# Layer 0's first gate and second scale vectors on TensorE, both first feed-forward chunks from x, and a GLA vector in the stage before

## The chip, the cores and the metric

One core of a Trainium2 chip runs the whole program. The engines are TensorE (PE, matrix products), VectorE (DVE), ScalarE (ACT), GpSimd (POOL) and SyncE (SP, whose queue issues the loads of weights). The metric is the device time of one execution in microseconds; lower is better. Products write to eight banks of PSUM, everything else lies in SBUF.

## The reference, cut to what matters

The model is a trunk of four residual layers for one sequence of 256 tokens of width 1024. Layers 0 and 3 mix tokens by sliding-window attention (16 query heads, 4 key heads), layer 1 by gated linear attention (GLA), layer 2 by forgetting attention. Each mixer is followed by a SwiGLU feed forward of width 2816. A vector `c` gives, per layer, six vectors of 1024: shift, scale and gate of the mixer, and shift, scale and gate of the feed forward.

```python
c_act = jax.nn.silu(c)
for i in range(DEPTH):
    mod = c_act @ ada_w[i] + ada_b[i]
    sh1, sc1, g1, sh2, sc2, g2 = jnp.split(mod, 6, axis=-1)
    h = modulate(rmsnorm(x, norm_gain[i, 0]), sh1, sc1)
    y = mixer(h)
    x = x + g1[:, None, :] * y
    h = modulate(rmsnorm(x, norm_gain[i, 1]), sh2, sc2)
    x = x + g2[:, None, :] * swiglu(h, ffn_w_gu[i], ffn_w_down[i])
return rmsnorm(x, final_norm)
```

`modulate(h, shift, scale)` is `h * (1 + scale) + shift`. All arrays are float32. In GLA each head's output of 256 columns is normalised by its own mean square before it is multiplied by a gate.

## The kernel before

**Layout.** `x` lies in SBUF with the features on partitions: eight tiles of 128 features by 256 tokens. A weight matrix comes in chunks of up to 1 MB, one DMA each, into one of five `raw` buffers. A chunk is then split into a high part `wh` (a cast on ACT, L194) and a low part `wl` (the rest, on DVE, L196), each in two pieces. The activations are split the same way (`hh`, `hl`), and a product is three matmuls, high x high, high x low and low x high (`mm3`, L277 to L279).

**The stream.** `Stream` holds one list of all chunks in the order in which they are loaded, the chunks of the `ada` matrices among them. It works through them in pieces. At every step of a product (`tick`) it does as many pieces as are due, so that the weights of the two chunks ahead (`LOOK`) are ready in time; an `ada` chunk that stands between weight chunks is worked off in its turn. A `raw` buffer is free for the next load when its last piece is done. A second generator (`bg`) feeds the steps of attention or GLA in between the same way. The order on each engine is that in which the code issues, as the framework's scheduler arranges it.

**The `ada` vectors.** A chunk gives two columns of `mod`, 256 of a vector's 1024 values. In general DVE does it: two dot products of 128x1024 with the spread-out `cact` (L213). For layer 0's first two vectors (shift and scale of the mixer) the matrix lies the other way round and PE does it in `ada_rows`: `product` multiplies with `ccol`, a column of `c` padded to 32, in eight matmuls of 128x32 by 256 columns (L228), ACT copies the resulting row (L229), and `turn` makes two columns of it with two matmuls (L233) to which DVE adds the bias (L235).

**Where the vectors stand in the stream.** `ORDER0` gives layer 0's order: h and s are shift and scale of the mixer, g its gate, H, S shift and scale of the feed forward, w a weight chunk. In the later layers `MIX_ADA` names the vectors that are loaded within the mixer, here number 4 (scale of the feed forward), and `DOWN_ADA` those that are loaded in the down projection before, number 2 (the mixer's gate); the rest goes into the gate-and-up chunks before.

**The output projection.** `out_proj` runs over two halves of the heads, in each over eight tiles of features. A tile takes a bank `mm` (three of them), twelve matmuls, and `add_x` on DVE (L514), which frees the bank.

**The feed forward's start.** The norm of `x` is not known until all of `x` is. `x_done` therefore forms, tile by tile, `uh` and `ul` = x times the norm's weights, and `first_chunk` multiplies the first chunk by these 256 columns and two of the shift; meanwhile the mean squares are summed (L326, L339), the reciprocal root is spread over partitions (L349), and `h_tiles` makes `hh` and `hl`. The result is scaled afterwards (L491). The second chunk comes from `hh` and `hl` (`proj_feat`).

**GLA.** `finish` squares a head's output on ACT into the two halves of `sq`, POOL adds the two halves (L1006), and PE sums over partitions (L1014).

## Time and profile before

| | |
|---|---|
| median of 3 runs | 1251.55 us (1249.82 to 1258.61) |
| profiled execution | 1254.5 us |
| its span, first to last instruction | 1252.7 us |
| mean granted TensorE clock | 0.987 |
| DMA | 298.51 MB, mean 238 GB/s |
| costliest DVE group, L196 `wl` | 448.4 us, 408 instructions |
| L213, the dot products of the `ada` vectors | 224.2 us, 176 instructions |

The profile gives busy time per engine, and for each idle stretch of an engine the instruction of another engine that ended it. A matmul's row in the timeline shows its length from start to end; since they overlap, the spacing of their starts tells what one costs in a row of them. `x4` at a row's end counts instructions that follow each other; a float32 matmul stands as two instructions. The windows view lists for each stretch the busy time of PE, PEld (weight loads), DVE, ACT and POOL, then the granted clock, the share of DMA time and GB/s.

### The profile page before, as it was taken

To read this page: it belongs to the slowest core of one execution; us is meant where nothing else is said; L and a number is where in the kernel's file an instruction comes from. 1 tells how busy PE (TensorE), PEld (TensorE's weight loads), DVE (VectorE), ACT (ScalarE), POOL (GpSimd) and SP (SyncE) were. 2 spreads that over 40 slices of the span, in tenths; PEclk is the share of its full clock that TensorE was granted. 3 is DMA by queue.
4 is the path that set the end of the run, shared out by engine and by line. 5 is a ranking of instruction groups with operands and counts; after the bars stand their busy time and mean duration, and the time that the engine had idled before them with its cause. 6 is when DMAs were issued, how large, how long until landed. Compare 5 with 4: busy or idle time off the path is not lost.

```text
span 1252.7 us, 19770 instructions
## 1 busy us (share of the span) xinstructions
PE 1207.5 (96%) x7444; PEld 1051.5 (84%) x7444; DVE 1001.1 (80%) x1828; ACT 697.8 (56%) x1293; POOL 133.9 (11%) x177
## 2 busy tenths in 40 slices
PE   6997899999998999999999999999999999999997
PEld 4875788888888998888889999888889979888886
DVE  3798998879779989888878668988787998666553
ACT  4474654444576666444457877645444677544442
POOL 0020110001115321000021101100011021000011
PEclk8998899999999999999999999999999999999999
DMA  9855789977744436998875543799788444656440
GB/s 355 330 196 206 269 295 347 344 269 261 267 175 162 165 137 233 355 331 292 272 270 200 202 173 132 278 351 343 266 279 280 166 153 169 225 212 214 161 163 34
DMA packets 45105, 298.51 MB, mean 238 GB/s; under 512 B 5217, under 2 KB 5377, under 8 KB 14802
## 3 DMA queue, kind: packets, MB, share of 16 engines
q1 hardware_dynamic: 44210, 295.56, 65.3%
q8 instruction: 58, 0.95, 0.3%
q10 hardware_dynamic: 432, 1.18, 0.3%
q0 software_dynamic: 368, 0.53, 0.1%
q14 instruction: 37, 0.30, 0.1%
HBM read 296.16 MB, written 1.05 MB: 237 GB/s over the span
## 4 chain that ended last, share of the span: by engine, by line
PE 85%; DVE 8%; ACT 3%; issue 2%; POOL 1%; DMA 1%; SPq 0%; DVEq 0%; ACTq 0%; POOLq 0%
PE mm L1160 13%; PE mm L277 12%; PE mm L278 12%; PE mm L279 11%; PE s L277 7%; PE s L278 7%; PE s L279 7%; PE mm L1162 7%; PE s L576 2%; DVE wl L196 2%; PE o L606 2%; DVE raw L213 2%; PE t L1131 1%; ACT wh L194 1%; PE t L617 1%
## 5 line engine op out<-in xcount | busy, mean ns | idle before, releaser
L196 DVE TENSOR_TENSOR wl<-raw,wh 128x1024 fp32r<-128x1024 f32 (+2 forms) x408 | 448.4, 1132 | 87.3 <-ACT wh L194 86.2
L194 ACT CAST wh<-raw 128x1024 fp32r<-128x1024 f32 (+2 forms) x408 | 375.9, 964 | 231.7 <-issue 105.1
L1160 PE MATMUL mm<-a,wh 128*128 128x512 f32 x704 | 247.8, 396 | 0.0
L213 DVE CUSTOM_DVE_ANT_0 raw<-raw,cact,const 128x1024 f32<-128x1024 f32 x176 | 224.2, 1292 | 16.7 <-DMA raw<-in_ada 16.5
L277 PE MATMUL mm<-wh,hh 128*128 128x512 f32 (+1 forms) x560 | 198.9, 355 | 2.2 <-ACT wh L194 1.8
L1162 PE MATMUL mm<-a,wl 128*128 128x256 f32 x704 | 198.0, 281 | 0.0
L278 PE MATMUL mm<-wl,hh 128*128 128x512 f32 (+1 forms) x560 | 194.9, 348 | 0.7 <-DVE wl L196 0.7
L279 PE MATMUL mm<-wh,hl 128*128 128x512 f32 (+1 forms) x560 | 194.6, 348 | 0.0
L1160 PEld LDWEIGHTS mm<-a,wh 128*128 128x128 f32 x704 | 132.2, 188 | 30.1
L277 PE MATMUL s<-wh,hh 128*128 128x512 f32 (+2 forms) x384 | 145.1, 379 | 2.9 <-ACT hh L454 2.9
L278 PE MATMUL s<-wl,hh 128*128 128x512 f32 (+2 forms) x384 | 143.2, 374 | 0.0
L279 PE MATMUL s<-wh,hl 128*128 128x512 f32 (+2 forms) x384 | 141.9, 373 | 0.0
L433 POOL TENSOR_TENSOR sq<-sq,sq 128x256 f32<-128x256 f32 x48 | 52.3, 1090 | 761.3 <-ACT sq L422 724.7
L1162 PEld LDWEIGHTS mm<-a,wl 128*128 128x128 f32 x704 | 133.0, 189 | 0.2
L277 PEld LDWEIGHTS mm<-wh,hh 128*128 128x128 f32 x560 | 107.1, 191 | 18.9 <-issue 3.0
L279 PEld LDWEIGHTS mm<-wh,hl 128*128 128x128 f32 x560 | 107.2, 191 | 13.9 <-issue 0.8
L278 PEld LDWEIGHTS mm<-wl,hh 128*128 128x128 f32 x560 | 107.2, 191 | 13.1 <-DVE wl L196 1.0
L514 DVE SCALAR_TENSOR_TENSOR x<-mm,mod,x 128x256 f32<-128x256 f32 x128 | 61.5, 481 | 42.9 <-PE mm L1162 35.2
L277 PEld LDWEIGHTS s<-wh,hh 128*128 128x128 f32 x384 | 72.3, 188 | 15.5 <-ACT hh L454 3.4
L277 PE MATMUL mm<-oh,wh 128*128 128x256 f32 x256 | 74.5, 296 | 9.3 <-DVE x L514 9.3
L279 PEld LDWEIGHTS s<-wh,hl 128*128 128x128 f32 x384 | 71.8, 188 | 13.1
L278 PEld LDWEIGHTS s<-wl,hh 128*128 128x128 f32 x384 | 72.3, 188 | 11.7
(220 smaller groups left out, 2005.7 us busy)
## 6 DMA issues: line engine op xcount, KB each, us to landing
raw<-in_ada SPq DMA_DIRECT2D x96, 1024.0 KB, 6.6
raw<-in_gu SPq DMA_DIRECT2D x88, 1024.0 KB, 6.1
raw<-in_down SPq DMA_DIRECT2D x64, 704.0 KB, 5.2
raw<-in_swa_in SPq DMA_DIRECT2D x12, 1024.0 KB, 6.6
raw<-in_gla_in SPq DMA_DIRECT2D x11, 1024.0 KB, 5.2
raw<-in_fox_in SPq DMA_DIRECT2D x11, 1024.0 KB, 4.9
raw<-in_swa_o SPq DMA_DIRECT2D x8, 1024.0 KB, 4.9
raw<-in_gla_o SPq DMA_DIRECT2D x4, 1024.0 KB, 4.9
```

Of the source, the lines that this page charges most:

```text
L194: nc.scalar.copy(wh[:, sl], raw[:, sl])
L196: eng.tensor_tensor(out=wl[:, sl], in0=raw[:, sl], in1=wh[:, sl].bitcast(F32), op=ALU.subtract)
L213: nc.vector.tensor_tensor_reduce(out=w, in0=w, in1=self.cact, scale=1.0, scalar=b, op0=ALU.mult, op1=ALU.add, accum_out=col)
L277: nc.tensor.matmul(out, ah, bh, start=first, stop=False)
L278: nc.tensor.matmul(out, ah, bl, start=False, stop=False)
L279: nc.tensor.matmul(out, al, bh, start=False, stop=last)
L433: (eng or nc.gpsimd).tensor_tensor(out=q, in0=self.acc, in1=q, op=ALU.add)
L514: self.nc.vector.scalar_tensor_tensor(out=self.x[:, m], in0=ps, scalar=gate[:, m:m + 1], in1=self.x[:, m], op0=ALU.mult, op1=ALU.add)
L576: nc.tensor.matmul(sc[:, so:s1], q[:, so:so + P], k[:, :k1], start=True, stop=True)
L606: nc.tensor.matmul(o[rows, b * P:S], vs[e][b], pt[:, e, :S] if b == 0 else pt[:, e, S:], start=b == 0, stop=b == 1)
L1160: nc.tensor.matmul(o, wh[:, k], a[:, kk].rearrange("p e n -> p (e n)"), start=kk == 0, stop=False)
L1162: nc.tensor.matmul(o[:, S:], wl[:, k], a[:, kk, 0], start=False, stop=kk == FT - 1)
```

## The change

It has four parts. `ROWS` extends `ada_rows` to layer 0's vectors 2 and 4 (first gate, second scale): their matrices are laid out like those of 0 and 1, and their chunks go through PE, in the mixer and the output projection, in a bank `mm` instead of `t`; `product` and `turn` are two pieces of the stream. `MIX_ADA` and `DOWN_ADA` become lists by layer: layer 1's vector 4 moves from GLA into layer 0's down projection, so SP issues its four loads there. `first_two` replaces `first_chunk` and `proj_feat` at the start of the feed forwards: both first chunks are multiplied by `uh` and `ul`, the mean squares are summed at the third step of the first chunk instead of the second, and the second half of `h_tiles` comes in the second chunk. In GLA POOL's sum goes, and PE adds both halves of the squares in one accumulation. The two attention masks become one table of four blocks in place of six, and a small tile shares the buffers of another; that makes room.

```diff
-MIX_ADA = (4,)
+MIX_ADA = ((), (), (4,), (4,))
-DOWN_ADA = (2,)
+DOWN_ADA = ((), (2, 4), (2,), (2,))
+ROWS = (0, 1, 2, 4)
...
-        if layer == 0 and nt < 2 * KT:
-            return self.ada_rows(mod[:, nt:nt + 2], bias[:, nt:nt + 2], raw)
+        if layer == 0 and nt // KT in ROWS:
+            return self.ada_rows(mod[:, nt:nt + 2], bias[:, nt:nt + 2], raw, nt < 2 * KT)
...
-        ps = self.ps("t")
-        row = self.t(self.small, [P, S], "fc", bufs=2)
+        ps = row = None
 
         def product():
+            nonlocal ps, row
+            ps = self.ps("t" if early else "mm")
+            row = self.t(self.small, [P, S], "fc", bufs=2)
...
-        return [product, lambda: self.turns.append(turn)]
+        return [product, (lambda: self.turns.append(turn)) if early else turn]
...
+    def first_two(self, names, use):
+        nc = self.nc
+        uh, ul = self.u
+        rbs = self.t(self.small, [P, S], "rbs", bufs=1)
+        for c, name in enumerate(names):
+            wh, wl = (x.rearrange("p (k n) -> p k n", k=KT) for x in self.st.get(name))
+            outs = [self.ps(("mm", "s")[c]) for _ in range(2)]
+            self.start_chunk(KT)
+            for k in range(KT):
+                for m in range(2):
+                    sl = slice(m * P, (m + 1) * P)
+                    self.mm3(outs[m][:, :S + 2], wh[:, k, sl], wl[:, k, sl], uh[:, k], ul[:, k],
+                             k == 0, k == KT - 1)
+                if c == 0 and k == 2:
+                    self.stat_start(self.acc)
+                    self.stat_end()
+                    nc.scalar.copy(rbs, self.spread(self.y))
+                    hh, hl = self.h_alloc()
+                    self.h_tiles(range(KT // 2), rbs, self.A, self.sh, hh, hl)
+                if c == 1 and k == 0:
+                    self.h_tiles(range(KT // 2, KT), rbs, self.A, self.sh, hh, hl)
+                self.tick()
+            vals = []
+            for m in range(2):
+                v = self.t(self.small, [P, S], "fc", bufs=2)
+                nc.vector.tensor_tensor(out=v, in0=outs[m][:, :S], in1=rbs, op=ALU.mult)
+                col = self.t(self.small, [P, 1], "fcol", bufs=4)
+                nc.vector.tensor_copy(col, outs[m][:, S:S + 1])
+                vals.append((v, col))
+            use(c, *vals)
+        return hh, hl
...
-            nc.gpsimd.tensor_tensor(out=sq[:, 0], in0=sq[:, 0], in1=sq[:, 1], op=ALU.add)
...
-                nc.tensor.matmul(st[:, b_:b_ + 1], sq[:, 0, b_ * P:(b_ + 1) * P],
-                                 self.c("ones")[:, 1:2], start=True, stop=True)
+                for hf in range(2):
+                    nc.tensor.matmul(st[:, b_:b_ + 1], sq[:, hf, b_ * P:(b_ + 1) * P],
+                                     self.c("ones")[:, 1:2], start=hf == 0, stop=hf == 1)
```

The next rows are DVE's order in layer 0's output projection, first half, before the change. `x_70` is x, `mod_5_74` layer 0's vectors; `L213` comes in pairs, the dot product and the read of its sum.

```order
L514 SCALAR_TENSOR_TENSOR x_70<-mm_1259,mod_5_74,x_70 128x256
L213 ISA raw_1023,mod_5_74<-raw_1023,cact_73,const_71 128x1024
L213 ISA mod_5_74 128x1
L213 ISA raw_1178,mod_5_74<-raw_1178,cact_73,const_71 128x1024
L213 ISA mod_5_74 128x1
L213 ISA raw_1178,mod_5_74<-raw_1178,cact_73,const_71 128x1024
L213 ISA mod_5_74 128x1
L514 SCALAR_TENSOR_TENSOR x_70<-mm_1278,mod_5_74,x_70 128x256
```

The same place after the change, where L214 is the dot product, L551 is `add_x`, L548 the low part of the heads' output and L238 the sum of a turned row.

```order
L238 TENSOR_TENSOR mod_5_74<-mm_1269,const_71 128x2
L551 SCALAR_TENSOR_TENSOR x_70<-mm_1290,mod_5_74,x_70 128x256
L214 ISA raw_1306,mod_5_74<-raw_1306,cact_73,const_71 128x1024
L214 ISA mod_5_74 128x1
L551 SCALAR_TENSOR_TENSOR x_70<-mm_1309,mod_5_74,x_70 128x256
L548 TENSOR_TENSOR ol_113<-o_1282,oh_112 128x256
L214 ISA raw_1306,mod_5_74<-raw_1306,cact_73,const_71 128x1024
L214 ISA mod_5_74 128x1
L551 SCALAR_TENSOR_TENSOR x_70<-mm_1331,mod_5_74,x_70 128x256
```

Between two `add_x` stands one dot product where three stood.

On PE at that place, before the change, there are the products of a tile and the transposes of attention (L617).

```order
L277 MATMUL mm_1259<-oh_112,wh_1017 128x256
L278 MATMUL mm_1259<-ol_113,wh_1017 128x256
L617 MATMUL t_1193<-const_71,pr_1135 128x128
L279 MATMUL mm_1259<-oh_112,wl_1018 128x256
L277 MATMUL mm_1259<-oh_112,wh_1017 128x256
```

After the change PE has there the product of a row (L231) and, behind five matmuls of the next tile, its turn (L236), which reads the copy `fc` that ACT makes in between.

```order
L282 MATMUL mm_1360<-oh_112,wl_1078 128x256
L231 MATMUL mm_1378<-raw_1238,ccol_97 32x256 x8
L280 MATMUL mm_1395<-oh_112,wh_1077 128x256
L281 MATMUL mm_1395<-ol_113,wh_1077 128x256
L282 MATMUL mm_1395<-oh_112,wl_1078 128x256
L280 MATMUL mm_1395<-oh_112,wh_1077 128x256
L281 MATMUL mm_1395<-ol_113,wh_1077 128x256
L236 MATMUL mm_1378<-const_71,fc_1379 128x1 x2
L282 MATMUL mm_1395<-oh_112,wl_1078 128x256
```

So a row stands between two tiles, and each row has its own place of the three banks `mm` from the product until the sum on DVE.

In layer 0's down projection DVE had this order before the change; `mod_6_75` are layer 1's vectors, 128x704 are the two pieces of a weight chunk.

```order
L196 TENSOR_TENSOR wl_2676<-raw_2540,wh_2675 128x704 x2
L514 SCALAR_TENSOR_TENSOR x_70<-mm_2628,mod_5_74,x_70 128x256 x2
L196 TENSOR_TENSOR wl_2713<-raw_2581,wh_2712 128x704 x2
L436 SCALAR_TENSOR_TENSOR ul_2590<-x_70,A_2587,uh_2589 128x256
L196 TENSOR_TENSOR wl_2751<-raw_2643,wh_2750 128x704 x2
L213 ISA raw_2726,mod_6_75<-raw_2726,cact_73,const_71 128x1024
L213 ISA mod_6_75 128x1
L213 ISA raw_2726,mod_6_75<-raw_2726,cact_73,const_71 128x1024
L213 ISA mod_6_75 128x1
```

After the change it is this (L197 is `wl`, L439 `ul`).

```order
L214 ISA raw_2822,mod_6_75<-raw_2822,cact_73,const_71 128x1024
L214 ISA mod_6_75 128x1
L439 SCALAR_TENSOR_TENSOR ul_2694<-x_70,A_2691,uh_2693 128x256
L197 TENSOR_TENSOR wl_2935<-raw_2838,wh_2934 128x704 x2
L214 ISA raw_2856,mod_6_75<-raw_2856,cact_73,const_71 128x1024
L214 ISA mod_6_75 128x1
L214 ISA raw_2856,mod_6_75<-raw_2856,cact_73,const_71 128x1024
L214 ISA mod_6_75 128x1
L551 SCALAR_TENSOR_TENSOR x_70<-mm_2883,mod_5_74,x_70 128x256
```

The dot products stand twice as close among the pieces of the weights.

More of the change, by code (lines that the diff above doesn't have):

```diff
@@ L38 @@
 CONST2_COLS = [
-    ("cos", NB * HD), ("sin", NB * HD), ("swamask", 3 * P), ("foxmask", 3 * P), ("scan", S),
+    ("cos", NB * HD), ("sin", NB * HD), ("masks", 4 * P), ("scan", S),
 ]
@@ L589, in attn_heads @@
                         nc.vector.tensor_tensor_reduce(
-                            out=sm[:, po:p1], in0=sc[:, so:s1], in1=mask[:, so:s1], scale=1.0,
+                            out=sm[:, po:p1], in0=sc[:, so:s1], in1=mask[:, 2 * P - (s1 - so):], scale=1.0,
                             scalar=BIG if ns is None else ns, op0=ALU.add, op1=ALU.min,
@@ L709, in head @@
             }
-        return self.attn_heads(pool, [head(h) for h in range(16)], self.c("swamask"), oh, ol)
+        return self.attn_heads(pool, [head(h) for h in range(16)], self.c("masks")[:, :2 * P], oh, ol)
     def pinned(self, start):
@@ L818, in few_cols @@
         nc = self.nc
-        t = self.t(self.small, [P, NB, 16], "few", bufs=1)
+        t = self.t(self.small, [P, S], "tk", bufs=3)[:, :NB * 16].rearrange("p (b n) -> p b n", b=NB)
         for b, ap in enumerate(parts):
@@ L838, in head @@
             }
-        gen = self.attn_heads(pool, [head(h) for h in range(16)], self.c("foxmask"), oh, ol)
+        gen = self.attn_heads(pool, [head(h) for h in range(16)], self.c("masks")[:, 2 * P:], oh, ol)
         for g in range(4):
@@ L1086, in gla, with gate_up_feat, use @@
         self.bg_rate = GLA_RATE[1]
-    def gate_up_feat(self, layer, j, pool, a):
+    def gate_up_feat(self, layer, pool, a):
         nc = self.nc
-        s = self.t(pool, [P, S], "st", bufs=2)
-        if j == 0:
-            self.hs, ((gv, gc), (uv, uc)) = self.first_chunk(f"g{layer}_0")
+        def use(j, gate, up):
+            (gv, gc), (uv, uc) = gate, up
+            s = self.t(pool, [P, S], "st", bufs=2)
             nc.scalar.activation(s, gv, AF.Silu, bias=gc)
             nc.vector.scalar_tensor_tensor(out=s, in0=uv, scalar=uc, in1=s, op0=ALU.add, op1=ALU.mult)
-        else:
-            g, u = self.proj_feat(self.st.get(f"g{layer}_{j}"), self.hs, "s")
-            nc.scalar.activation(s, g, AF.Silu)
-            nc.vector.tensor_tensor(out=s, in0=s, in1=u, op=ALU.mult)
-        self.split_hl(s, a[:, j, 0], a[:, j, 1], nc.gpsimd)
+            self.split_hl(s, a[:, j, 0], a[:, j, 1], nc.gpsimd)
+        self.hs = self.first_two([f"g{layer}_0", f"g{layer}_1"], use)
     def gate_up_tok(self, layer, g, pool, a, before):
@@ L1141, in ffn @@
             a = self.t(pool, [P, FT, 2, S], "a", F32R)
-            for j in range(2):
-                self.gate_up_feat(layer, j, pool, a)
+            self.gate_up_feat(layer, pool, a)
             turn = None
@@ L1232, in items @@
                 items += mix[:MIX_SPAN[0]]
-                d = sum((ada(l, v) for v in MIX_ADA), [])
+                d = sum((ada(l, v) for v in MIX_ADA[l]), [])
                 if l + 1 < DEPTH:
@@ L1239, in items @@
             if l + 1 < DEPTH:
-                done = MIX_ADA + (MIX_NEXT if l else ())
-                d1 += sum((ada(l + 1, v) for v in (1, 0, 2, 3, 4) if v not in done + DOWN_ADA), [])
-                d2 = sum((ada(l + 1, v) for v in DOWN_ADA), [])
+                done = MIX_ADA[l + 1] + DOWN_ADA[l + 1] + (MIX_NEXT if l else ())
+                d1 += sum((ada(l + 1, v) for v in (1, 0, 2, 3, 4) if v not in done), [])
+                d2 = sum((ada(l + 1, v) for v in DOWN_ADA[l + 1]), [])
             items += ff[:3]
@@ L1348, in _layout @@
     a["ada"] = ada.reshape(DEPTH * 6, 4, 2, P, D).transpose(0, 1, 3, 2, 4).reshape(DEPTH * 6, 4, P, 2 * D)
-    for v in range(2):
+    for v in ROWS:
         a["ada"][v] = _chunks(i["ada_w"][0, :, v * D:(v + 1) * D], 256)
@@ L1401, in _layout @@
     caus, full = off(kj <= qi), np.zeros((P, P), f)
-    put("swamask", np.concatenate([caus, off(kj > qi), caus], 1))
-    put("foxmask", np.concatenate([caus, full, caus], 1))
+    put("masks", np.concatenate([off(kj > qi), caus, full, caus], 1))
     put("scan", np.tile((np.arange(S) % 64 != 0).astype(f)[None], (P, 1)))
```

2 lines of the change are left out of this document (1 added, 1 removed).

## The prediction

> **What bounds the kernel now.** I read the page first, then windows of 10 us over the whole span, then the list of waits in the stretches where TensorE (PE) is not full, then the timeline there.
>
> ```profile
> span 1252.7 us, 19770 instructions
> PE 1207.5 (96%) x7444; PEld 1051.5 (84%) x7444; DVE 1001.1 (80%) x1828; ACT 697.8 (56%) x1293; POOL 133.9 (11%) x177
> PE   6997899999998999999999999999999999999997
> PEclk8998899999999999999999999999999999999999
> ```
>
> PE is the bound: it is idle for 1252.7 - 1207.5 = 45.2 us in all. So an edit can gain only where PE waits or its granted clock is down, and PE work that is added costs its full time wherever PE is full. Of the stretches that the change touches, the windows give this (columns: length, busy time of PE, PEld, DVE, ACT, POOL, granted clock, DMA share, GB/s):
>
> ```profile
> 60.10:144.20 84.10, 70.62 (x499) 57.63 (x497) 75.96 (x199) 50.78 (x138) 14.41 (x33) 0.92 0.62 226
> 984.50:1052.70 68.20, 66.87 (x532) 57.20 (x531) 61.81 (x178) 51.68 (x140) 13.77 (x33) 1.00 0.48 171
> 282.50:341.00 58.50, 57.77 (x353) 51.49 (x351) 49.52 (x74) 29.87 (x48) 7.17 (x8) 1.00 0.79 281
> 340.00:480.00 140.00, 130.58 (x1038) 125.11 (x1037) 122.44 (x289) 97.11 (x180) 36.43 (x38) 1.00 0.43 150
> ```
>
> The first is layer 0's attention and output projection, from the first transposes of the keys to the first product of its feed forward. The second is the same stretch of layer 3, which runs the same code. The third is layer 0's down projection with GLA's first chunk, the fourth GLA. In layer 0 PE is idle for 13.5 us and its clock is down for part of the rest:
>
> ```profile
> PE mm L277 <- DVE x L514: 9.4, 5, 2.6
> PE t L679 <- ACT wh L194: 3.2, 1, 3.2
> 98.00:100.00 2.00, 2.00 (x7) 1.02 (x7) 2.00 (x7) 0.69 (x2) 0.00 (x0) 0.50 0.93 393
> 134.00:136.00 2.00, 2.00 (x11) 2.00 (x11) 1.61 (x3) 1.29 (x4) 0.24 (x1) 0.50 0.98 356
> ```
>
> The large wait is for `add_x` (L514), which frees the `mm` bank that PE wants; behind it and behind the wait of 3.2 us the clock is at half. What holds VectorE (DVE) up is the dot product of the scale vectors, L213. This is its busy time in layer 3's and in layer 0's stretch (half of the instructions are the read of the accumulator):
>
> ```profile
> 984.50:1052.70 68.20, 8.99 (x14) 1.00 0.48 171
> 60.10:144.20 84.10, 27.57 (x44) 0.92 0.62 226
> ```
>
> **Layer 0's gate and second scale on PE.** Sixteen of layer 0's 24 pieces of L213 leave DVE, and eight remain, about what layer 3 has (7 in its stretch). So layer 3 shows what the stretch costs with that much DVE work. By the order of the program it has 36 more products in it (chunks that layer 0 does earlier), at the spacing of the rows below, 0.12 us: 4.3 us. Layer 0 at layer 3's pace takes 68.2 - 4.3 = 63.9 us, against 84.1: an excess of 20.2 us, which is waits, half clock and the disorder behind both. Against it stands what PE gets: eight products of 8 matmuls and eight turns of 2, which the kernel already does for the first two vectors (the first two rows are of the chain of waits, the others of the timeline; the last two are `add_x` and a piece of L213):
>
> ```profile
> 40.05 1.00 PE t L228 x16
> 41.05 0.54 PE t L233 x4
> 39.65 0.28 PE L278 MATMUL mm<-wl,hh 128*128 128x256 f32 x1
> 39.77 0.28 PE L279 MATMUL mm<-wh,hl 128*128 128x256 f32 x1
> 39.98 1.07 PE L228 MATMUL t<-raw,ccol 128*32 128x256 f32 x16
> 40.22 0.36 ACT L229 COPY fc<-t 128x256 f32<-128x256 f32 x1
> 40.98 1.14 PEld L233 LDWEIGHTS t<-const,fc 128*128 128x128 f32 x8 [0.41 <-ACT fc L229]
> 279.79 0.48 DVE L514 SCALAR_TENSOR_TENSOR x<-mm,mod,x 128x256 f32<-128x256 f32 x1 [1.43 <-PE mm L1162]
> 337.78 1.28 DVE L213 CUSTOM_DVE_ANT_0 raw<-raw,cact,const 128x1024 f32<-128x1024 f32 x1 [0.76 <-DMA raw<-in_ada]
> ```
>
> A product takes 1.00 and a turn 0.54 us. The first matmul of the product starts 0.21 us after the one ahead of it where 0.12 is usual, so entering costs 0.1 and I take as much for leaving: 1.74 us a row, 13.9 for eight. [...]
>
> That leaves 20.2 - 13.9 = 6.3 us at most. Two things take from it. Six of the eight remaining pieces stand in the first half of the output projection, one between two `add_x`; at 1.28 us and 0.48 each they take DVE some 1.7 us a tile while PE needs 12 x 0.12 = 1.43, some 0.25 x 5 = 1.2 us. And a turn waits for ACT's copy of the row; it stands five matmuls (0.6 us) or more behind its product and the copy takes 0.36, so I take 0.5 us for all eight. On DVE the turns add eight adds of two columns, on ACT eight copies, 2.9 us; both engines have room (76 - 20 of 84 us, 51 of 84). Gain 4.6. Ends: 6.3, and a loss of 0.4 if the excess only falls as the pieces do (two thirds of 20.2, 13.5, against 13.9). I take the value near the upper end because layer 3's row is the same code.
>
> **GLA's matrix a stage earlier.** Four loads (8 pieces of L213) go from GLA into layer 0's down projection, on SP's queue and on DVE. GLA's waits, with what PE waits for:
>
> ```profile
> PE t L1014 <- POOL zz L1006: 1.6, 3, 1.0
> PE s L277 <- ACT hh L454: 1.5, 1, 1.5
> PE o L999 <- ACT at L992: 1.4, 1, 1.4
> PE mm L279 <- DVE wl L196: 1.3, 1, 1.3
> PE s L919 <- DVE at L982: 1.0, 1, 1.0
> 386.31 1.66 DVE L213 CUSTOM_DVE_ANT_0 raw<-raw,cact,const 128x1024 f32<-128x1024 f32 x1
> 407.21 1.32 DVE L213 CUSTOM_DVE_ANT_0 raw<-raw,cact,const 128x1024 f32<-128x1024 f32 x1
> L1014 PE MATMUL t<-const,zz 128*128 128x1 f32 x16 | 2.3, 250 | 1.6 <-POOL zz L1006 1.6
> ```
>
> The wait of 1.5 us for `hh` stands behind the piece at 337.78, which DVE issues ahead of the tiles of `h`: 0.8 goes. The waits for `at` L992 and for `wl` follow the pieces at 386 and 407: I take 1.2 and 1.1. The wait for POOL's sum of squares goes with it, 1.6, and 0.9 of the smaller rest: 5.6 in all. The sum on PE is eight more matmuls of one column; by the row (2.3 us for 16 instructions) 16 more of about 0.12 take 1.9. Gain 3.7. Ends: all idle time of the window, 9.4 - 1.9 = 7.5; and none but POOL's, 1.6 - 1.9, a loss of 0.3.
>
> **What the moved loads meet.** The window of the down projection has DVE at 49.5 of 58.5 us; one moved piece is in it already, seven more make 58.5, all of it. Two chunks of weights are prepared ahead (2 x 3.8 us), which covers a lag of a few us. But DVE works in order and already waits for these loads:
>
> ```profile
> 281.69 1.29 DVE L213 CUSTOM_DVE_ANT_0 raw<-raw,cact,const 128x1024 f32<-128x1024 f32 x1 [1.41 <-DMA raw<-in_ada]
> 295.92 1.29 DVE L213 CUSTOM_DVE_ANT_0 raw<-raw,cact,const 128x1024 f32<-128x1024 f32 x1 [2.25 <-DMA raw<-in_ada]
> DMA packets 2619, 16.50 MB, mean 280 GB/s; under 512 B 290, under 2 KB 290, under 8 KB 1334
> ```
>
> The window moves 16.5 MB; four more loads make 20.7 MB in 58.5 us, 354 GB/s, which the rows at 98 and 134 us reach. I take 1.0 us: `wl` queues behind a waiting piece, PE behind `wl`. Ends: nothing, and 5 us, the two waits doubled (3.7) and 1.3 that DVE then lacks.
>
> **Feed forwards' second chunk from x.** Four times 48 products go from 256 to 258 columns, at the same spacing; DVE gets about 1 us more per feed forward and half of the `h` tiles move a chunk later. What PE waits for at the four starts is this:
>
> ```profile
> 144.40 0.39 PE L277 MATMUL mm<-uh,wh 128*128 128x258 f32 x1 [0.16 <-DVE x L514]
> 146.56 0.61 PE L326 MATMUL t<-const,sq 128*128 128x1 f32 x4 [0.59 <-POOL sq L433]
> 467.14 0.39 PE L277 MATMUL mm<-uh,wh 128*128 128x258 f32 x1 [0.63 <-DVE x L514]
> 776.65 0.39 PE L277 MATMUL mm<-uh,wh 128*128 128x258 f32 x1 [0.54 <-DVE x L514]
> 1053.68 0.39 PE L277 MATMUL mm<-uh,wh 128*128 128x258 f32 x1 [0.49 <-DVE x L514]
> ```
>
> No row has PE waiting for `h` there, so the deadline that is lifted was not binding. The waits for L514 belong to the output projection and stay. Only the 0.59 us for POOL can go, since the sums stand a step later: gain 0.3, ends 0.75 and a loss of 0.5 (the added DVE work late for the third chunk's `wl`). The merged masks and the shared small tile change no instruction's size on the path: nothing.
>
> **Sum.** -4.6 - 3.7 - 0.3 + 1.0 = -7.6 us. The profiled execution took 1254.5 us (1252.7 and 1.8 around it), 2.95 above the median of 1251.55: 1246.9 for it, 1244.0 for the median.
>
> **Rivals.** (a) All waits go: 6.3 + 7.5 + 0.75 = 14.6 us, 1237. For it speaks that layer 3 runs its stretch with 1.3 us idle; against it that GLA's waits for L982 at 1.0 us and others have no piece of L213 ahead of them. (b) GLA's waits are the length of its chain from engine to engine, not DVE's queue: the pieces go, the waits stay, GLA gives -0.3 and the sum is -3.6: 1248. For it speaks that PE waits on five different producers there; against it the pieces just ahead of three of the waits. (c) Slower: the turns. PE runs in order, and the turn of a row waits for ACT's copy. In layer 0 ACT has weight casts in pairs of 2.0 us:
>
> ```profile
> 95.58 1.99 ACT L194 CAST wh<-raw 128x1024 fp32r<-128x1024 f32 x2
> ```
>
> A copy behind such a pair makes PE wait 1.99 + 0.36 - 0.6 = 1.75 us; at all eight turns 14.0 in place of my 0.5, so the sum is +5.9 and the time 1257.5. It decides the sign from 1.0 us a turn ((7.6 + 0.5) / 8). For it speaks the 0.41 us that the quoted turn's weight load waited for the copy; against it that ACT is busy 51 of 84 us there. (d) The moved loads lame the down projection at their upper end, 5 us in place of 1: 1248, the same as (b).
>
> **How the numbers follow.** My forecast (1240.5 to 1247) has 0.52, (a) 0.17, (b) and (d) together 0.20, (c) 0.11. The predicted time is 1244.0. A range from 1237 to 1252 holds the forecast, (b) and (d) and the near half of (a), and leaves out (c) and the far half of (a), about 0.2. A measurement tells about 1% of this kernel, 12.5 us, from no change: below 1239.0 lies most of (a), 0.15; above 1264 only the far end of (c), 0.02; 0.83 within.
>
> **What would show it.** Right: in the stretch from the keys' transposes to the first feed-forward product (84.1 us now) about 79.5, the clock at 1.00 throughout, the wait for L514 below 2 us, turns that wait below 0.1 us on average; GLA some 3.7 us shorter than its 140, with no wait at the sum of squares; the down projection with DVE near 100% and PE waits for `wl` of about 1 us; the four starts unchanged. Wrong: rows that cost PE more than 1.74 us, waits at the turns, DVE waiting for `in_ada` more than 4 us in the down projection and PE behind it, or GLA with the same waits on other names.

## The result, and the profile after

| | before | after |
|---|---|---|
| median | 1251.55 us (7 runs) | 1245.91 us (1243.52 to 1246.55, 7 runs) |
| ratio to before | | 0.9928, 95% interval 0.9905 to 0.9952 |
| profiled execution, its span | 1254.5, 1252.7 us | 1244.97, 1243.2 us |
| mean granted clock | 0.987 | 0.994 |

The medians differ by 5.6 us, the two profiled spans by 9.5. The profiled execution of before lay 2.95 us above its median and that of after 0.9 below, which makes up the difference. The page of after begins thus (span, busy time by engine, PE and its clock in 40 slices):

```profile
span 1243.2 us, 20119 instructions
PE 1213.5 (98%) x7620; PEld 1056.1 (85%) x7620; DVE 985.1 (79%) x1820; ACT 701.3 (56%) x1301; POOL 125.7 (10%) x173
PE   6999999999998999999999999999999999999997
PEclk8999999999999999999999999999999999999999
```

PE has 6.0 us more to do and is idle for 29.7 us where it was idle for 45.2. The slices 3 to 5 (62 to 155 us), with most of layer 0's attention and output projection, are full where they read 9, 7 and 8 before, and by this row the clock is down in the first slice alone. The windows show where the time went. The marks are the same in both programs: the first transposes of the keys, the first product of a feed forward, the first product of a down projection, GLA's first product, its output projection. First before (layer 0's stretch, its down projection, GLA), then after:

```profile
60.14:143.71 83.57, 70.09 (x496) 57.28 (x495) 75.43 (x198) 50.29 (x137) 14.32 (x32) 0.92 0.63 228
271.50:332.98 61.48, 61.48 (x358) 54.15 (x357) 49.52 (x70) 32.14 (x50) 5.75 (x6) 1.00 0.79 279
332.98:439.91 106.93, 98.42 (x785) 94.41 (x783) 92.74 (x225) 73.68 (x139) 31.20 (x33) 1.00 0.48 169
```

```profile
59.16:135.17 76.01, 75.80 (x636) 60.13 (x635) 58.76 (x176) 53.37 (x145) 13.17 (x33) 1.00 0.62 240
263.26:325.31 62.05, 62.05 (x358) 54.25 (x356) 57.72 (x85) 32.37 (x50) 5.46 (x6) 1.00 0.95 343
325.31:432.24 106.93, 100.84 (x797) 97.24 (x796) 82.00 (x208) 73.29 (x139) 25.02 (x30) 0.98 0.36 129
```

Layer 0's stretch is 7.56 us shorter. In it PE waits for 0.2 us where it waited for 13.5, the clock is 1.00, and DVE has 58.8 us of work in place of 75.4. The down projection with the moved loads is 0.57 us longer, with PE full and DVE at 57.7 of 62.05. GLA has the same length to the hundredth: PE waits less in it (106.93 - 100.84 = 6.1 us in place of 8.5), does 2.4 us more, and its clock is 0.98. Of the rest of the 9.5 us, the stage ahead of the stretch gives 1.0, layer 1's feed forward 1.6, and the others, the 0.57 among them, take back 0.6. Of the 1.6, its down projection gives 1.0: it took 63.07 us before, where layers 0 and 2 took 61.5, and 62.06 after.

In GLA these are the waits of PE after the change (what waits, for whom, us, times, longest):

```profile
PE o L1036 <- ACT at L1029: 1.8, 1, 1.8
PE s L956 <- DVE at L1025: 1.5, 2, 0.8
PE t L352 <- DVE y L371: 1.3, 2, 0.7
PE mm L282 <- DVE wl L197: 0.7, 1, 0.7
PE s L956 <- DVE qz L994: 0.6, 1, 0.6
PE s L956 <- DVE at L1019: 0.2, 1, 0.2
```

L1036 is L999 of before, L956 is L919, L352 is L349, L282 is L279. The waits for `hh` and for POOL are gone. The others stand there on the same names, longer or in other places, though no dot product runs in GLA any more.

### The profile page after: what moved, and what is told of

It reads as the page before. It is cut to its first block, busy times and chain, and to the rows that moved or that the text cites. A ratio compares the mean times of both kernels' runs of the same rounds, so it can differ in the third digit from the quotient of the medians.

```text
span 1243.2 us, 20119 instructions
## 1 busy us (share of the span) xinstructions
PE 1213.5 (98%) x7620; PEld 1056.1 (85%) x7620; DVE 985.1 (79%) x1820; ACT 701.3 (56%) x1301; POOL 125.7 (10%) x173
## 4 chain that ended last, share of the span: by engine, by line
PE 88%; DVE 5%; ACT 4%; issue 1%; POOL 1%; DMA 0%; SPq 0%; DVEq 0%; ACTq 0%; POOLq 0%
PE mm L1194 13%; PE mm L280 12%; PE mm L281 12%; PE mm L282 12%; PE s L282 7%; PE s L280 7%; PE s L281 7%; PE mm L1196 7%; PE s L613 2%; PE o L643 2%; DVE wl L197 1%; PE t L1166 1%; PE t L654 1%; ACT wh L195 1%; PE s L956 1%
## 5 line engine op out<-in xcount | busy, mean ns | idle before, releaser
L197 DVE TENSOR_TENSOR wl<-raw,wh 128x1024 fp32r<-128x1024 f32 (+2 forms) x408 | 446.2, 1123 | 85.9 <-ACT wh L195 84.9
L214 DVE CUSTOM_DVE_ANT_0 raw<-raw,cact,const 128x1024 f32<-128x1024 f32 x160 | 204.1, 1291 | 3.7 <-DMA raw<-in_ada 3.5
L282 PE MATMUL mm<-wh,hl 128*128 128x512 f32 (+1 forms) x560 | 194.0, 346 | 0.0
L282 PE MATMUL s<-wh,hl 128*128 128x512 f32 (+2 forms) x384 | 142.3, 374 | 0.0
L280 PEld LDWEIGHTS mm<-wh,hh 128*128 128x128 f32 x560 | 106.4, 190 | 19.4 <-issue 3.1
L282 PEld LDWEIGHTS mm<-wh,hl 128*128 128x128 f32 x560 | 106.3, 190 | 13.9 <-issue 0.5
L281 PEld LDWEIGHTS mm<-wl,hh 128*128 128x128 f32 x560 | 106.4, 190 | 13.3 <-DVE wl L197 1.0
L551 DVE SCALAR_TENSOR_TENSOR x<-mm,mod,x 128x256 f32<-128x256 f32 x128 | 61.4, 480 | 41.9 <-PE mm L1196 32.3
L282 PEld LDWEIGHTS s<-wh,hl 128*128 128x128 f32 x384 | 71.6, 188 | 13.3 <-DVE hl L450 0.2
L281 PE MATMUL mm<-ol,wh 128*128 128x256 f32 x256 | 73.6, 288 | 0.0
```

The costliest lines, as they stand in the source:

```text
L197: eng.tensor_tensor(out=wl[:, sl], in0=raw[:, sl], in1=wh[:, sl].bitcast(F32), op=ALU.subtract)
L214: nc.vector.tensor_tensor_reduce(out=w, in0=w, in1=self.cact, scale=1.0, scalar=b, op0=ALU.mult, op1=ALU.add, accum_out=col)
L280: nc.tensor.matmul(out, ah, bh, start=first, stop=False)
L281: nc.tensor.matmul(out, ah, bl, start=False, stop=False)
L282: nc.tensor.matmul(out, al, bh, start=False, stop=last)
L551: self.nc.vector.scalar_tensor_tensor(out=self.x[:, m], in0=ps, scalar=gate[:, m:m + 1], in1=self.x[:, m], op0=ALU.mult, op1=ALU.add)
```

## The experiments

Twelve kernels ran. All are the change with one edit unless said otherwise. The ratio is to the kernel before on the same chip; e1 to e4 ran on one chip, e5 to e8 on a second, e9 to e11 on a third, and e12 by itself. "Stretch" is layer 0's from the keys' transposes to the feed forward, "half clock" the time that PE lost there (busy time times what the granted clock lacked, summed over windows of 1 us), all in us.

| kernel | median | ratio, 95% interval | stretch | PE idle in it | half clock |
|---|---|---|---|---|---|
| before | 1251.55 | | 83.57 | 13.5 | 5.3 |
| the change | 1245.91 | 0.9928 (0.9905 to 0.9952) | 76.01 | 0.2 | 0 |
| e1, no new rows | 1248.90 | 0.9956 (0.9938 to 0.9974) | 82.33 | 12.8 | 4.2 |
| e2, old feed-forward start | 1246.98 | 0.9945 (0.9923 to 0.9967) | 75.99 | 0.2 | 0 |
| e3, vector back in GLA | 1247.51 | 0.9937 (0.9915 to 0.9960) | 75.99 | 0.2 | 0 |
| e4, POOL's sum back | 1247.17 | 0.9946 (0.9926 to 0.9965) | 75.99 | 0.2 | 0 |
| e5, before plus the rows | 1247.77 | 0.9946 (0.9925 to 0.9968) | 75.79 | 0.2 | 0 |
| e6, shift on PE too | 1251.91 | 0.9981 (0.9964 to 0.9998) | 82.38 | 0.2 | 0 |
| e7, rows for the gate alone | 1242.07 | 0.9903 (0.9880 to 0.9926) | 74.01 | 5.5 | 2.6 |
| e8, rows for the scale alone | 1245.76 | 0.9932 (0.9911 to 0.9955) | 77.11 | 2.7 | 0 |
| e9, gate and half the scale | 1238.07 | 0.9886 (0.9865 to 0.9907) | 69.66 | 0.2 | 0 |
| e10, gate, other vectors spread | 1242.63 | 0.9920 (0.9902 to 0.9938) | 74.04 | 6.0 | 0 |
| e11, products in two pieces | 1242.26 | 0.9926 (0.9902 to 0.9949) | 73.29 | 0.0 | 0 |
| e12, e9 with slower GLA steps | 1239.86 | 0.9885 (0.9855 to 0.9916) | 69.71 | 0.2 | 0 |

The stretch is much steadier than the medians: five kernels with the change's order in it took 75.79 to 76.01 us. The stage ahead of it, in which all these kernels have nearly the same work to do, took 57.65 to 64.82 us. So the experiments on one stage are read from that stage.

**Without the new rows (e1).** The gate and the second scale are dot products on DVE again; all else is the change.

```diff
-ROWS = (0, 1, 2, 4)
+ROWS = (0, 1)
```

> The changed kernel with layer 0's gate and second scale back on DVE (ROWS = (0, 1)), all else as changed. Theory: the rows give the gain, because DVE's dot products held up add_x and the weights. Then layer 0's stretch from the keys' transposes to the first feed-forward product goes from 76.0 back to about 83.6 us with half clock in it, and the median is 1252 to 1255 us. Rival: the stretch became shorter through the other order that the scheduler made of the program; then it stays below 79 us and the median below 1249.

The stretch went back to 82.3 us, with the waits that the change had removed:

```profile
57.73:140.06 82.33, 69.49 (x497) 57.05 (x496) 75.51 (x198) 50.38 (x137) 14.72 (x32) 0.94 0.64 231
...
PE mm L280 <- DVE x L551: 9.2, 4, 2.6
PE t L716 <- ACT wh L195: 3.2, 1, 3.2
```

Nine microseconds for `add_x`, 3.2 for `wh`, and a lowered clock behind them: the same two rows as before the change. So the rows, and nothing else of the change, remove them. PE is busy for 69.5 us, 65.3 at full clock, where the change has 75.8: its rows, seven of which lie in the stretch (the first lies ahead of the keys' transposes), cost 10.5 us, 1.5 each. The median missed its forecast: 1248.90 us lies below the 1252 to 1255 of the theory, on the rival's side. By the ratios, 0.9956 against 0.9928, the rows are worth 0.28%, 3.5 us, where the stretch has 6.3. In the profiled execution the start and layer 0's gate-and-up stage were 1.4 and 1.2 us shorter than with the change.

**The rows alone (e5).** The kernel before, with `ada_rows`, `ROWS` and the layout of the two matrices as in the change.

```diff
+ROWS = (0, 1, 2, 4)
...
-        if layer == 0 and nt < 2 * KT:
+        if layer == 0 and nt // KT in ROWS:
...
```

> The kernel before with the rows for layer 0's gate and second scale on PE as its only change. Theory: it has the whole gain of layer 0's stretch, 7.5 us there and nothing elsewhere: 1243 to 1245.5 beside 1251.5. Rival: the parts need each other (the stretch is shorter only with the other order of the feed forward's start): less than 4 us of gain.

The stretch took 75.79 us with 0.2 us of waits: the rows alone give the gain of this stage. The median is above the forecast's 1245.5, but on this chip the kernel before took 1254.36 us, so the gain is 6.6 us. By the ratios the rows give 0.54% of the change's 0.72% here, and 0.28% by e1; these two estimates differ by no more than the intervals allow, so the medians do not tell how the gain divides between the rows and the rest.

**All four later vectors on PE (e6).**

```diff
-ROWS = (0, 1, 2, 4)
+ROWS = (0, 1, 2, 3, 4)
```

> The changed kernel with the second shift on PE too, four more rows. PE has 0.2 us of idle time in layer 0's stretch, so nothing is left to win and the stretch shows the price of a row. By the forecast's 1.74 us it is 7.0 us longer (83.0), by the busy time of the rows in the changed kernel's profile (9.8 and 4.2 us for eight, with overlap) 1.4 us each, 5.6 us longer. If the eight pieces that are left on DVE still cost PE time, it is less than 4 us longer.

```profile
57.65:140.03 82.38, 82.23 (x716) 63.59 (x715) 50.86 (x164) 55.08 (x149) 11.78 (x33) 1.00 0.60 223
```

There was no wait left for four more rows to remove, so they cost their full price: 82.23 - 75.80 = 6.43 us, 1.61 a row. The ratio is back at 0.998.

**Gate alone, scale alone (e7, e8).**

```diff
-ROWS = (0, 1, 2, 4)
+ROWS = (0, 1, 2)
```

> The changed kernel with only the gate on PE, the second scale on DVE (eight pieces come back to DVE, four rows leave PE). If DVE's queue costs PE time in proportion to its pieces, the waits return by half (3.5 to 4 us) and the rows' price goes (5.6 to 7): the stretch is 2 to 3 us shorter than 76.0. If the queue has a threshold, since the second scale's pieces stand close together in the output projection, PE waits there 3 to 5 us and the clock falls: the stretch is 0 to 3 us longer.

The second kernel has `ROWS = (0, 1, 4)`.

> The changed kernel with only the second scale on PE, the gate on DVE. The gate's pieces stand in the projection part, where DVE has more room than in the output projection: the stretch is 2 to 3 us shorter than 76.0 by both theories, since the dense place in the output projection is relieved. If PE instead waits for a late gate (the output projection needs it to begin), the stretch is longer than 76.0.

```profile
61.50:135.51 74.01, 68.47 (x557) 57.73 (x555) 66.28 (x187) 51.16 (x140) 13.81 (x32) 0.95 0.66 244
...
61.18:138.29 77.11, 74.39 (x576) 58.31 (x575) 66.56 (x186) 51.98 (x141) 12.68 (x32) 1.00 0.65 243
```

The first line is of e7, the second of e8. Gate rows alone are 2.0 us better than the change, as the first expectation had it, but with the waits (5.4 us for `add_x`) and the half clock of the second. Scale rows alone are 1.1 us worse, where 2 to 3 us better were expected. Both have four new rows, yet PE is busy for 8.5 us less at full clock in e7 (68.5 - 2.6 = 65.9 against 74.4), of which the one row of e7 that lies ahead of the mark explains 1.5. The timeline shows what differs: the small tiles (the rows' products of 128x32, the P x V products of attention of 128x64) stand together in e7 and are broken up in e8. First e7 (start, length, instruction):

```profile
76.56 1.07 PE L231 MATMUL mm<-raw,ccol 128*32 128x256 f32 x16
77.56 0.93 PE L613 MATMUL s<-uh,qT 64*128 64x128 f32 x8
...
87.88 0.87 PE L643 MATMUL o<-pt,v 128*64 128x256 f32 x8
88.68 0.38 PE L280 MATMUL mm<-wh,hh 128*128 128x256 f32 x1
```

Then e8:

```profile
84.08 0.62 PE L231 MATMUL mm<-raw,ccol 128*32 128x256 f32 x2
84.63 0.66 PE L716 MATMUL t<-const,qr 128*128 128x128 f32 x4
85.21 1.06 PE L231 MATMUL mm<-raw,ccol 128*32 128x256 f32 x14
86.21 0.39 PE L280 MATMUL mm<-wh,hh 128*128 128x256 f32 x1
86.52 0.65 PE L643 MATMUL o<-pt,v 128*64 128x256 f32 x2
87.10 0.93 PE L613 MATMUL s<-uh,qT 64*128 64x128 f32 x8
87.95 0.86 PE L643 MATMUL o<-pt,v 128*64 128x256 f32 x6
88.75 0.44 PE L654 MATMUL t<-const,pr 128*128 128x128 f32 x2
```

Reckoned from a start to the next, a whole product takes 1.00 us (76.56 to 77.56) and a broken one 0.55 + 1.00 (84.08 to 84.63, 85.21 to 86.21): a break costs 0.55. A whole group of P x V takes 0.80 and a broken one 0.58 + 0.80. The framework's scheduler decides where other tiles get in, and every edit of the stream shuffles that. Summed over the stretch (number of groups, time from each start to the next start, us; eight groups of P x V and one of each row would be whole):

| kernel | rows in it | their products | P x V |
|---|---|---|---|
| e1 | 0 | | 11 groups, 8.8 (0.7 of it by half clock) |
| the change | 7 | 9 groups, 8.1 | 10 groups, 8.3 |
| e6 | 11 | 16 groups, 13.3 | 10 groups, 7.6 |
| e7 | 3 | 3 groups, 3.0 | 9 groups, 6.8 |
| e8 | 4 | 8 groups, 5.8 | 12 groups, 9.7 |
| e9 | 5 | 6 groups, 5.6 | 9 groups, 6.8 |
| e11 | 7 | 13 groups, 8.2 | 8 groups, 6.6 |

Between e7 and e8 the rows' breaks are worth 1.8 us and those of P x V 2.9, and the row more 1.5: 6.2 of the 8.5 us; the rest is not accounted for. So a row's price of 1.5 to 1.6 us, read from e1, the change and e6, is a mean in which breaks are contained; one that stands whole costs 1.00 and some 0.43 for its turn (three turns in e7 took 1.29).

**Gate and half of the second scale (e9).** If a gate row is cheap and waits come only where three or more dot products stand between two `add_x`, then the last two chunks of the scale should go to PE and the rest stay on DVE.

```diff
-ROWS = (0, 1, 2, 4)
+ROWS = (0, 1, 2)
...
-        if layer == 0 and nt // KT in ROWS:
+        if layer == 0 and (nt // KT in ROWS or nt in (4 * KT + 4, 4 * KT + 6)):
...
+    a["ada"][4, 2:] = _chunks(i["ada_w"][0, :, 4 * D:5 * D], 256)[2:]
```

> Rows for the gate (four) and for the last two chunks of the second scale (two); two chunks of the scale stay on VectorE. Theory (a row costs PE 1.0 + 0.54 us where its matmuls stand together, and 0.55 more where another tile breaks into them; a wait for add_x appears only behind three or more dot products in a row): the order has no place with more than one dot product between two add_x of the output projection. So the stretch is that of the gate rows alone, 74.0 us, less its 5.5 us of waits and 2.5 us of half clock, plus two rows, 3.1 us, and one break, 0.6: about 69.7, at most 71.5, clock 1.00. Rival (the wait falls in proportion to the dot products, whatever their places): half way between gate rows and all four rows of the change, 75.0 us.

```profile
58.30:127.96 69.66, 69.43 (x596) 57.45 (x595) 61.88 (x181) 51.62 (x142) 13.95 (x32) 1.00 0.71 264
```

The stretch took 69.66 us, full and at full clock, 6.35 less than with the change, and the median of 1238.07 is the best of the study, 1.1% below before (interval 0.9865 to 0.9907); the change stands at 0.9928, with an interval that begins at 0.9905, so the two just overlap. e12, which has the same order in this stage, took 69.71 us. So two of its eight rows were better left on DVE. Of the 6.35 us, the rows' products give 2.5 and their turns 1.0; P x V, which stands in fewer groups, gives 1.5, and the rest is in other products and transposes. That part of the gain is the scheduler's order and was not forecast.

**The other vectors spread (e10).** Rows for the gate alone, as in e7, and the chunks of the shift and the scale ahead of the last three chunks of the output projection as 2, 3, 3 in place of 1, 2, 5.

```diff
-ORDER0 = "shwshshwshwwwgwwgggSwHSwHSSHHw"
+ORDER0 = "shwshshwshwwwgwwgggSHwSHSwHSHw"
...
-ROWS = (0, 1, 2, 4)
+ROWS = (0, 1, 2)
```

> Rows for the gate alone, and the chunks of shift and second scale spread as 2, 3 and 3 ahead of the last three chunks of the output projection instead of 1, 2 and 5. Theory (the wait comes from dot products that stand three and more in a row): two stand between add_x at most, 3.5 us of VectorE against 1.43 us of PE, so a wait stays, but each shorter: the sum falls from 5.4 to about 3 us and the clock loss with it; the stretch is 71 to 73 us. Rival (VectorE's sum of work in the output projection decides, not its order): 74.0 us as with the gate rows alone.

Here the theory failed, and with it the premise of e9 that a wait needs three dot products in a row; e9's 69.7 us came true without it. The waits became shorter but more, and the stage kept its length:

```profile
PE mm L280 <- DVE x L551: 5.9, 5, 1.6
62.41:136.45 74.04, 68.08 (x557) 55.85 (x555) 66.63 (x187) 51.26 (x140) 13.40 (x32) 1.00 0.68 245
```

In e7 it was 5.4 us in three waits, the longest 2.3. Without the long wait the clock stayed at 1.00, which saved 2.6 us, but P x V cost 0.8 more with one break more, and the rest of PE's work too. The rival had the number right (DVE's work in the output projection decides, not its order); what became of the 2.6 us was only read from the groups, not tested.

**Products in two pieces (e11).** The change, with four matmuls of a product in one piece of the stream and four in the next.

```diff
...
-        return [product, (lambda: self.turns.append(turn)) if early else turn]
+        if early:
+            return [lambda: (product(), rest()), lambda: self.turns.append(turn)]
+        return [product, rest, turn]
```

> The change, with the product of a row issued as two pieces of four matmuls, so that other tiles of PE come between them. Theory (a group of small tiles that is broken costs PE about 0.55 us more): seven rows lie in the stretch and two of them were broken already, so five new breaks, 2.8 us: the stretch goes from 76.0 to about 78.8 us at clock 1.00 without waits, the median 2 to 3 us up. Rival (the price belongs to the matmuls, not to their neighbours): 76.0 within 0.4 us.

Both expectations missed: the stretch became 2.7 us shorter.

```profile
64.82:138.11 73.29, 73.29 (x636) 58.66 (x635) 57.91 (x175) 52.16 (x144) 11.27 (x32) 1.00 0.68 252
```

By the table the rows' products stand in 13 groups in place of 9 and cost only 0.1 us more. Two halves apart take 0.57 us each where the whole takes 1.00, so a break between the halves costs 0.14; the break of e8 that cost 0.55 stood behind the first of the eight matmuls. P x V lost both of its breaks and 1.7 us, and the large products became 1.2 us shorter, 0.2 of it idle time. What an edit does to the neighbours' order can outweigh what it does itself.

**The old start of the feed forward (e2).** `first_chunk` and `proj_feat` as before the change.

```diff
...
-            self.gate_up_feat(layer, pool, a)
+            for j in range(2):
+                self.gate_up_feat(layer, j, pool, a)
```

> The changed kernel with the second feed-forward chunk from h again. Theory: the deadline that was lifted was not binding, so the time stays within 1 us of 1245.9 and each feed forward's gate-and-up part within 0.3 us. Rival: the chunk from x gives 0.5 us in each of the four feed forwards (the parts of layers 1 to 3 are 0.5 us shorter after the change); then 1247.5 to 1248.5.

The gate-and-up stages of layers 1, 2 and 3 went from 126.86, 126.78 and 126.68 us to 127.13, 127.16 and 127.01, so `first_two` gives 0.3 us in each, between the theory and the rival. Before the change these stages took 127.42, 127.30 and 127.26 us, so another 0.1 to 0.3 us came from elsewhere. The down projections did not change. Layer 0's stage, 1.8 us longer, had its clock lowered in part.

**The vector back in GLA (e3) and POOL's sum back (e4).**

```diff
-MIX_ADA = ((), (), (4,), (4,))
-DOWN_ADA = ((), (2, 4), (2,), (2,))
+MIX_ADA = ((), (4,), (4,), (4,))
+DOWN_ADA = ((), (2,), (2,), (2,))
```

> The changed kernel with layer 1's fourth vector back in GLA (four loads, eight pieces on DVE). Theory one, DVE's queue: GLA to the first product of its feed forward (133.1 us after the change) gets 3 us longer, layer 0's down projection (62.0 us) 0.6 shorter: 1248. Theory two, GLA's waits are the length of its chain from engine to engine: GLA stays within 1 us at equal clock, the time within 1 us of 1245.9.

e4 has the addition on POOL and one matmul a block again.

```diff
+            nc.gpsimd.tensor_tensor(out=sq[:, 0], in0=sq[:, 0], in1=sq[:, 1], op=ALU.add)
...
-                for hf in range(2):
-                    nc.tensor.matmul(st[:, b_:b_ + 1], sq[:, hf, b_ * P:(b_ + 1) * P],
-                                     self.c("ones")[:, 1:2], start=hf == 0, stop=hf == 1)
+                nc.tensor.matmul(st[:, b_:b_ + 1], sq[:, 0, b_ * P:(b_ + 1) * P],
+                                 self.c("ones")[:, 1:2], start=True, stop=True)
```

> The changed kernel with POOL's sum of the squares in GLA again. Theory: the wait of PE for POOL comes back (1.6 us) and 1.5 us of products go: GLA within 0.5 us at equal clock, 1245.5 to 1246.5 in all. Rival: POOL's sum delays the decays that follow it on POOL, and GLA is 1.5 us longer or more.

First e3's down projection of layer 0 and its GLA, then GLA and its first wait in e4:

```profile
266.51:328.56 62.05, 62.05 (x357) 54.18 (x356) 50.02 (x72) 31.96 (x50) 7.44 (x6) 1.00 0.80 277
328.56:437.98 109.42, 102.73 (x797) 98.83 (x795) 91.23 (x225) 73.82 (x139) 30.55 (x30) 0.97 0.47 165
```

```profile
326.19:434.29 108.10, 99.97 (x785) 96.02 (x784) 82.43 (x208) 73.27 (x139) 27.34 (x33) 0.98 0.36 128
PE t L1051 <- POOL zz L1043: 2.3, 2, 1.7
```

GLA's lengths have to be read at equal clock, that is with the time lost at half clock taken out. Its rows show 1.00 in some kernels, 0.98 in others and 0.97 here, which is none, one or two stretches of 3.4 us at half clock, 1.7 us of loss each by PE's busy time. So GLA is 106.0 us in e3, 106.4 in e4 and 105.2 in the change: the vector's eight dot products would cost GLA 0.8 us, and POOL's sum 1.2. The nine kernels with the change's GLA allow a comparison without this subtraction: they took 105.40 to 105.58 us with no such stretch (e2, e6, e8, e10), 106.92 or 106.93 with one (the change, e1, e7, e11) and 108.26 with two (e9). So one costs 1.3 to 1.5 us, and beside kernels with as many, e3 and e4 are both 1.2 us longer. The two do not add up: e5, which has the vector and POOL's sum in GLA, is only 0.3 us longer than the change with one stretch each. POOL's sum cost more than the theory's 0.5 us and less than the rival's 1.5. The down projection in e3 is 62.05 us without the moved loads as with them: what the move costs there is nothing.

**GLA's steps slower (e12).** e9 with

```diff
-GLA_RATE = (0.585, 2.55)
+GLA_RATE = (0.54, 2.55)
```

> The kernel with rows for the gate and half of the second scale, and GLA's steps at a rate of 0.54 a product step in place of 0.585. Theory (GLA's waits are the length of its chain from engine to engine): thirteen products stand between two steps where seven to thirteen stood, so PE's waits for the chain (L956 and L1036, 4.1 us together) fall to 2 us or less and GLA's idle time from 5.9 to about 4; the stage at equal clock goes from 104.9 to about 103 us, if the steps that come later don't lengthen the output projection behind it (26.2 us). Rival (VectorE's load in the stage sets them, which the edit doesn't change): idle 5.9 and 104.9 at equal clock within 0.3 us.

PE's waits in GLA, where e9 has the same list as the change but 0.5 for `wl`:

```profile
PE o L1036 <- DVE at L1025: 2.2, 1, 2.2
PE t L352 <- DVE y L371: 1.0, 2, 0.7
PE mm L282 <- DVE wl L197: 0.7, 1, 0.7
PE s L956 <- DVE qz L994: 0.6, 1, 0.6
PE t L1051 <- ACT zz L1042: 0.6, 1, 0.6
```

The waits for the chain at L956 and L1036 fell from 4.1 to 2.8 us with DVE's load hardly changed (82.8 us busy, 82.1 in e9), two of those at L956 are gone, and GLA at equal clock went from 104.9 to 103.9; beside the kernels with one stretch of half clock, like its own, its 105.60 us are 1.3 less than 106.93. That is half of what was expected or somewhat more, and the output projection behind it grew by 0.2, but the sign is that of a chain whose steps come too early for their producers. The ratio did not move (0.9885).

## Why the prediction was right, and where its steps were wrong

The predicted 1244.0 us lies 1.9 below the measured median, and the change lies within 1% as forecast. Its terms were less good than their sum: layer 0's was 3 us too small and GLA's up to 3.4 too large. That the two nearly cancel is luck.

**Layer 0's gate and second scale: right in mechanism, too small.** The forecast had a gain of 4.6 and the stage gave 7.56. That the dot products hold up `add_x` and so PE, with half clock behind, is shown by e1 and e5: with the rows off both waits are back, with the rows alone both are gone. Several sizes were off. The two deductions (1.2 us for the pieces left in the output projection, 0.5 for the turns) did not occur: PE's idle time in the stretch is 0.2 us. A row cost 1.5 to 1.6 in place of 1.74. And one of the eight rows lies ahead of the stretch. DVE's dot products in the stretch fell as forecast to layer 3's level:

```profile
59.16:135.17 76.01, 10.25 (x16) 1.00 0.62 240
```

The layer 3 comparison, an excess of 20.2 us, was close: idle time and half clock of before are 13.5 + 5.3 = 18.8 us, of which 0.2 stayed, and PE's added work took 75.80 - (70.09 - 5.3) = 11.0. So 18.6 - 11.0 = 7.6 stands where the forecast had 20.2 - 13.9 - 1.7 = 4.6.

A row that stands whole cost 1.43 us in e7 with its turn (1.00 + 0.43), so the sum's 1.74 was too high for such a row. Why a broken group costs more, 0.55 us for a break in e8 and 0.14 in e11, no run here shows.

**GLA: the step that failed.** The forecast gave 3.7 us; the profiled stage gave nothing, and at equal clock 1.7 us against the profile of before (some 1.5 by the four kernels without half clock in GLA). It read three of five waits as DVE's queue because a dot product stood ahead of them. Two of them fell with the dot products: `hh` (1.5 us, which comes back as 2.0 in e3) and part of `wl` (1.3 to 0.7). The waits at the steps of the chain did not: they stand at L956, L1036 and L352 with no dot product in the stage. So what the moved vector was worth is 0.8 to 1.2 us by e3, where the step had some 4. POOL's wait went, with 0.9 us more work on PE (100.84 - 99.97) where 1.9 was taken, a gain of 1.2 by e4 where the step had a loss of 0.3. This is rival (b)'s mechanism for most of GLA's waits, and e12 bears it out, since later steps alone took the waits at L956 and L1036 from 4.1 to 2.8 us; its total of 1248 did not come, since layer 0 gave more. How well 1.7 us is known must be said too: e5 runs GLA as before did, and its stage is 107.19 us with one half-clock stretch:

```profile
323.57:430.76 107.19, 99.75 (x784) 95.69 (x783) 92.99 (x225) 73.68 (x139) 31.81 (x33) 0.98 0.47 168
```

That is 105.5 at equal clock against before's 106.9, with nearly the same order of instructions on every engine; PE's wait for POOL's sum is 1.4 us in before and 0.3 in e5. Why they differ is open. So GLA's gain lies between 0.3 and 1.7 us, and where in between is not settled; the 0.8 and 1.2 us of e3 and e4, single profiles too, are no better known.

**The moved loads: 1.0 us forecast, nothing found.** The stage did grow by 0.57, with DVE at 57.7 of 62.05 us and 343 GB/s, close to the 354 reckoned. But e3 has the same 62.05 with the loads elsewhere, and layer 2's down projection, where nothing was moved, grew as much. Before and after:

```profile
902.89:964.36 61.47, 61.47 (x358) 54.14 (x357) 49.68 (x70) 31.87 (x50) 7.82 (x6) 1.00 0.81 277
```

```profile
893.42:955.48 62.06, 62.06 (x358) 54.24 (x356) 50.03 (x70) 31.84 (x50) 7.13 (x6) 1.00 0.78 273
```

PE is full in both with the same count of matmuls: each of the 176 pairs stands 3.3 ns further from the next (0.59 us / 176). e5, which has neither the new mask table nor the shared small tile, kept 61.46 in layer 0; every kernel with them had 62.05 or 62.06. Here the forecast's "merged masks and the shared small tile: nothing" is the likelier culprit, by what differs; they were not tried alone, nor why they would matter. One more stage of each of the two kernels without them stands apart, layer 1's in before with 63.07 us and layer 2's in e5 with 62.93; no kernel with them has such a stage, and its cause is open.

**Feed forwards' second chunk: too small, and for another reason.** A gain of 0.3 was forecast for all four starts together, 0.75 at most; e2 shows 0.3 in each of three layers, 1.0 in sum. The forecast took it from the wait for POOL in layer 0, which still takes 0.5 us there. In layers 1 to 3 PE has the same single wait, for `add_x`, in e2 and in the change, so where the 0.3 comes from is open.

**Rivals.** (c), turns that wait for ACT's copy, did not occur: there is no wait at a turn in the stretch. (d), the moved loads, did not occur. (a) needed GLA's waits to go, and 6.1 us of idle time are left there.

## What to carry to other kernels

Where one engine's side work delays a freed buffer, moving just enough of it off that engine is better than moving all: here 16 dot products fewer brought 7.6 us, 12 fewer and the matching six rows brought 13.9; 1.5 us of the difference lie in a better order of attention's products. The small matmul tiles were cheaper here where they stood together (a product of a row 1.00 us whole in e7, 1.55 with the break in e8, 1.14 in two halves in e11); look at the scheduled order for broken groups before pricing such a move, since the edit also reshuffles its neighbours (in e11 P x V lost both of its breaks and 1.7 us). A wait that follows a busy instruction on the producer's engine is not yet caused by it: take that instruction away first, by an edit or in thought, and see whether the chain would be ready.
